# Attention's last product with one mask, gates in other tiles, pinned table loads and earlier kept weights in a two-layer hybrid kernel

## The chip, the cores and the metric

The kernel runs on one core of one Trainium2 chip. The metric is device time in microseconds (us) of the one launch. Engines are named as in the profile: PE (TensorE) does matrix products and transposes, PEld its weight loads, DVE is VectorE, ACT is ScalarE, POOL is GpSimd, SP is SyncE, which here does little but issue DMAs, in the order in which they stand in its program.

## The reference

One sequence of 512 tokens and width 1024 goes through two hybrid layers and one second block, all in float32. Cut to what matters here:

```python
def hybrid_layer(x, ...):
    h = rmsnorm(x, pre_mix_g)
    (dn_q, dn_k, dn_v, dn_z, dn_b, dn_a, sw_q, sw_k, sw_v,
     gate_a, gate_b) = jnp.split(h @ w_in, IN_OFFSETS, axis=-1)
    y_a = deltanet_branch(...) @ w_up_dn          # its output is gated by silu(z) as well
    y_b = swa_sink_branch(sw_q, sw_k, sw_v, positions, sw_sinks) @ w_up_sw
    mix = (sigmoid(gate_a) * y_a + sigmoid(gate_b) * y_b) @ w_o
    x = x + rmsnorm(mix, post_mix_g)
    h2 = rmsnorm(x, pre_mlp_g)
    ff = square(relu(h2 @ w_ff1)) @ w_ff2         # 4096 hidden
    return x + rmsnorm(ff, post_mlp_g)

# swa_sink_branch: 16 query heads, 2 key heads of 64, blocks of 128 tokens;
# every block sees itself and the block before it
off = qi - ki
in_band = (off >= 0) & (off < 128)
probs = p / (sum(p) + exp(sink - m))
o = einsum('bnhgqk,bnkhd->bnqhgd', probs, v_of_both_blocks)

# second block, state-space branch: tables of each group from parameters
dt = exp(log_dt); mag = exp(lam_re * dt); ang = lam_im * dt
bbar = coef(lam_re, lam_im, mag, ang) * (b_re, b_im)
```

The band has one property that the change uses: for a query row, the keys of the own block that are allowed (at or before it) and the keys of the block before that are allowed (after its place there) are complements. With the scores of both put in one 128-wide row, one probability matrix P holds both parts, and a mask says which part an entry belongs to.

## The kernel before

The token axis is the free axis of the products, and the 1024 channels lie as eight blocks of 128 partitions. Every float32 product is done as three matmuls on numbers split into a high and a low half (`mm3`; all matmuls are recorded at L78, transposes at L81). A weight block of 128x1024 is loaded by SP into a raw tile (`raw` has 2 buffers, `rawx` 1, `raws` its own), cast to its high half (`wh`, or `kw` where the block is kept for both halves of the tokens) by ACT at L241 or L221 (by POOL at L239), and the low half is a subtraction on DVE at L242 or L222.

A scheduler puts the instructions of each engine in an order, by costs that it estimates; an instruction passed to `tc.keep_in_program_order` keeps its place in the order in which the code is written. Each engine then works strictly in its order, and so does SP's queue of DMAs.

The stages of a layer that the change touches:

- Attention, L928 to L1025, a generator for each query block `b` and key head `kv`, run beside the projections. After the softmax (exponentials at L995, the scaling `sc` by `den` at L999), four heads at a time are transposed on PE and copied by ACT to `pc` (L1007). For b>0 POOL makes two masked copies of it, `pv` (L1010) for the values of the block before and `pc` in place (L1012) for the own values, and PE adds two products.
- Mix. For each of eight output blocks n, a load of the delta rule's output (`ogf`) and of its gate 0 (`gate`) from DRAM (`fetch`, L1315), their product on DVE (L1335), the split into `ah` (ACT L336, DVE L339); and the product of attention's output with `w_up_sw`, times gate 2 (L1340, `tb`). `ogf`, gate 0 and gate 2 take turns in one ring of three tiles ("fe"). Then follow the eight products that take all `ah`, with `w_up_dn`. Where a gate is not yet activated, ACT does it at L1321.
- Feed-forward. Its first product runs in two halves of 256 tokens; the residual and its norm are finished beside it (`xo` loads at L430, `xd_mid` stores at L401, `rt` on DVE and POOL at L432 and L433, `xsh`/`xsl` at L341/L342, squares summed in `sa` at L365/L370). The hidden blocks get relu and square on ACT (`ft` L1380, `fq` L1382) and a split (`hh` L336, `hl` L339). Beside it run `token_sums` (`tsa`, `tsb`) and `ssm_tables`, which loads the parameters of half of the second block's groups (`row` L1059, `dt` L1067, `lbr` and `lbi` L1072, `crow` L1105) and works out tables.
- Feed-forward's end. The last quarter of `w_ff2` is applied half by half: blocks 0 to 2 first by `halves3`, the other five by `dense_half`, each added to `acc` (L1490); the weights `kw` are kept for the second half.

Of the kernel before, what the change touches and what calls it, by code (L numbers as in the profile page):

```python
# [9 lines left out]
F32 = mybir.dt.float32  # L10
# [4 lines left out]
ALU = mybir.AluOpType  # L15
# [4 lines left out]
P = 128  # L20
# [3 lines left out]
KD = D // P  # L24
# [30 lines left out]
def body(  # L55
# [27 lines left out]
    T = Tensor()  # L83
# [16 lines left out]
    def rest(n):  # L100
        for _ in range(n):
            yield
# [119 lines left out]
            V.tensor_tensor(out=lo, in0=t, in1=f32(h), op=ALU.subtract)  # L222
            return h, lo

    def load_w(src, kn=KD, n=P, pool_h=False, keep=None):
        turn[0] += 1
        if turn[0] % 3 == 2 and turn[1] is not None and turn[0] > turn[2]:
            raw = turn[1].tile([P, kn, n], F32, tag="rawx", name="rawx", bufs=1)
        else:
            raw = wp.tile([P, kn, n], F32, tag="raw", name="raw", bufs=2)  # L230
        DMA.dma_start(out=raw, in_=src.rearrange("(k p) n -> p k n", p=P))
        h = lo = None
        if keep is not None:
            h, lo = keep(kn, n), keep(kn, n)
        if h is None:
            h = wp.tile([P, kn, n], F32R, tag="wh", name="wh", bufs=3)
            lo = wp.tile([P, kn, n], F32R, tag="wl", name="wl", bufs=3)
        if pool_h:
            G.tensor_scalar(out=h, in0=raw, scalar1=1.0, scalar2=0.0, op0=ALU.mult, op1=ALU.add)  # L239
        else:  # L240
            S.copy(out=h, in_=raw)  # L241
        V.tensor_tensor(out=lo, in0=raw, in1=f32(h), op=ALU.subtract)  # L242
        return h, lo

# [682 lines left out]
    def sw_item(l, b, kv, qk, vt, sw, kts, db):  # L927
# [70 lines left out]
        V.reciprocal(out=den, in_=den)  # L998
        V.tensor_tensor(out=sc, in0=sc, in1=den.unsqueeze(3).to_broadcast([P, 2, 4, P]), op=ALU.mult)  # L999
        yield from rest(PRB)  # L1000
        pcs = []
        for o in range(2):
            ps = ps_ax()
            for i in range(4):
                T.transpose(ps[:, i, :], sc[:, o, i, :], ident)
            pc, pv = sw.tile([P, 4, P], F32, tag="pc", name="pc", bufs=2), None
            S.copy(out=pc, in_=ps)  # L1007
            if b:
                pv = sw.tile([P, 4, P], F32, tag="pv", name="pv", bufs=2)
                G.affine_select(out=pv, in_=pc, pattern=[[0, 4], [-1, P]], base=0, channel_multiplier=1,  # L1010
                                compare_op=ALU.is_gt, fill=0.0)
            G.affine_select(out=pc, in_=pc, pattern=[[0, 4], [1, P]], base=0, channel_multiplier=-1,  # L1012
                            compare_op=ALU.is_ge, fill=0.0)
            pcs.append((pc, pv))
        yield from rest(PV)
        po = ps_ax()
        for o, (pc, pv) in enumerate(pcs):
            hs = slice(64 * o, 64 * o + 64)
            dst = po[hs].rearrange("p h t -> p (h t)")
            if b:  # L1020
                T.matmul(dst, lhsT=vt[:, b - 1, kv * 64:kv * 64 + 64], rhs=pv.rearrange("p h t -> p (h t)"), start=True, stop=False)
            T.matmul(dst, lhsT=vt[:, b, kv * 64:kv * 64 + 64], rhs=pc.rearrange("p h t -> p (h t)"), start=not b, stop=True)
        of = r2("sof")
        V.tensor_copy(out=of, in_=po)
        DMA.dma_start(out=db[:, 4 * kv:4 * kv + 4, b * P:(b + 1) * P], in_=of)  # L1025
# [20 lines left out]
    def ssm_tables(sp, hf):  # L1046
# [6 lines left out]

        prs = slice(NG * hf, NG * hf + NG)
        grs = slice(2 * NG * hf, 2 * NG * hf + 2 * NG)
        lam = {}
        for nm, src in (("lr", ssm_lam_re_2), ("li", ssm_lam_im_2)):
            row = sp.tile([NG, P], F32, tag="row", name="row")
            DMA.dma_start(out=row, in_=src[0, grs].rearrange("(i two) p -> i (two p)", two=2))  # L1059
            ps = ps_ax((P, NG))  # L1060
            T.transpose(ps, row, ident[:NG, :NG])
            lam[nm] = tl(nm)
            V.tensor_copy(out=lam[nm], in_=ps)
        lr, li = lam["lr"], lam["li"]
        dt = tl("dt")
        for half in range(2):
            DMA.dma_start(out=dt[64 * half:64 * half + 64, :],  # L1067
                          in_=ssm_log_dt_2[0, grs].rearrange("(i two) -> two i", two=2)[half].partition_broadcast(64))
        bre, bim = tl("lbr", (P, NG, 2, 16))[:, :, 0, :], tl("lbi", (P, NG, 2, 16))[:, :, 0, :]
        for dst, src in ((bre, ssm_b_re_2), (bim, ssm_b_im_2)):  # L1070
            for half in range(2):
                DMA.dma_start(out=dst[64 * half:64 * half + 64],  # L1072
                              in_=src[0, grs].rearrange("(i two) p c -> two p i c", two=2)[half])
        yield

# [26 lines left out]
        for src in (ssm_c_re_2, ssm_c_im_2):  # L1102
            crow = sp.tile([P, 2, 2, 64], F32, tag="crow", name="crow", bufs=2)
            for dup in range(2):
                DMA.dma_start(out=crow[:, :, dup, :], in_=src[0, grs].rearrange("(q g) c p -> (g c) q p", q=2))  # L1105
            crows.append(crow)
        s16 = (P, NG, 16)
        tC, tD = tl("tC", s16), tl("tD", s16)
# [83 lines left out]
    def layer(l, st, nxt):  # L1192
# [111 lines left out]
        with sbuf(f"mx{l}") as mp:  # L1304
            third(mp)
            def m2(name, dtype=F32R):
                t = mp.tile([P, 2, SEQ], dtype, tag="m2", name=name, bufs=NM2)
                return t[:, 0, :], t[:, 1, :]

            def keep(kn, n):  # L1310
                return mp.tile([P, kn, n], F32R, tag="m2", name="kw", bufs=NM2)

            def fetch(src, n, name):
                t = mp.tile([P, SEQ], F32, tag="fe", name=name, bufs=3)
                DMA.dma_start(out=t, in_=src[:, n, :])  # L1315
                return t

            def gate(i, n):
                t = fetch(dg[i], n, "gate")
                if (i, n) in plain:  # L1320
                    S.activation(out=t, in_=t, func=gate_fn[i])  # L1321
                return t

            bo, ao = [], []
            for n in range(KD):
                hl = m2("bh")
                split(*hl, fetch(db, n, "bf"), eng=G)
                bo.append(hl)
            tb = []
            for n in range(KD):  # L1330
                if n % 2 == 0:
                    pair = m2("tb", F32)
                w = load_w(w_up_sw[l][:, n * P:(n + 1) * P])
                t = fetch(og, n, "ogf")
                V.scalar_tensor_tensor(out=t, in0=t, scalar=pcol("dn_norm", l), in1=gate(0, n), op0=ALU.mult, op1=ALU.mult)  # L1335
                hl = m2("ah")
                split(*hl, t)
                ao.append(hl)
                ps = dense(w, bo)
                V.tensor_tensor(out=pair[n % 2], in0=ps, in1=gate(2, n), op=ALU.mult)  # L1340
                tb.append(pair[n % 2])
            mix = []
            for n in range(KD):
                ps = dense(load_w(w_up_dn[l][:, n * P:(n + 1) * P]), ao)
                ta_ = gate(1, n)
                V.tensor_tensor(out=ta_, in0=ps, in1=ta_, op=ALU.mult)
                V.tensor_tensor(out=ta_, in0=ta_, in1=tb[n], op=ALU.add)
                hl = m2("mh")
                split(*hl, ta_)
                mix.append(hl)  # L1350
            mo = [mt.tile([P, SEQ], F32, tag="mo", name="mo", bufs=KD) for _ in range(KD)]
            mid = Stream("pre_mlp", l * KD, f"xd_mid{l}", mt, False)
            wk, tick = {}, None
            for i in range(2):
                ms = Stats(mt)
                for n in range(KD):
                    if i == 0:
                        wk[n] = load_w(w_o[l][:, n * P:(n + 1) * P], keep=keep if n >= 3 else None)
                    ps = dense_half(wk[n], mix, i)
                    V.tensor_copy(out=mo[n][:, HALVES[i]], in_=ps)  # L1360
                    ms.add(mo[n][:, HALVES[i]])
                    if i:
                        tick()
                pending = residual(st, mo, ms.rstd, "post_mix", l * KD, mid, i)
                if i == 0:
                    before = pending
                    tick = ticks(before, AT_O)
            finish(before)

        with sbuf(f"ff{l}") as ff, ExitStack() as es2:  # L1370
# [109 lines left out]
            for i in range(2):  # L1480
                fs = Stats(tr)
                for n in range(KD):
                    if i == 0 and n == 0:
                        wk = {j: w.take() for j in range(3)}
                        head = halves3([wk[j] for j in range(3)], i)
                    elif i == 0 and n >= 3:
                        wk[n] = load_w(down(3, n)[0], keep=keep)
                    ps = head[n] if i == 0 and n < 3 else dense_half(wk[n], hid, i)
                    ac = acc[n][:, HALVES[i]]
                    V.tensor_tensor(out=ac, in0=ps, in1=ac, op=ALU.add)  # L1490
                    fs.add(ac)
                    if i:
                        tick()
# [275 lines left out]
```

## Time and profile before

| | us |
|---|---|
| median of 3 runs | 2309.17 (2308.73 to 2314.07) |
| the profiled execution | 2315.69 |
| its span, first to last instruction | 2313.9 |
| PE busy in it | 2243.0 (97%) |
| DVE busy | 1485.3 (64%) |
| ACT busy | 952.1 (41%) |
| POOL busy | 609.4 (26%) |
| DMA queue of SP (q1), share of 16 engines | 41.9% |

The profiled execution is 6.52 us longer than the median of the runs; 1.79 us of it lie outside the span. PE is the engine to look at: its weight loads overlap its matmuls, so its time is lost in two ways only, as idle time in front of an instruction that waits, and as stretches in which the granted clock is 0.5 of full speed (mean over the span 0.982).

### The profile page before, as it was taken

The numbers are of one execution on the slowest core, as the hardware profiler recorded it, in microseconds if no ns is written. First come the engines' busy times: TensorE is split into PE (matmuls) and PEld (weight loads), VectorE is DVE, ScalarE is ACT, GpSimd is POOL, SyncE is SP. The second block draws the span as 40 slices with busy tenths as digits, with TensorE's granted clock in tenths as the row PEclk, the third lists the DMA queues.
The fourth block names the chain that finished last, engine by engine and source line by source line (L and its number), as shares of the span: only waits on it lengthen the run. The fifth ranks groups of instructions, "written<-read, shape, count | busy, mean of one in ns | idle before, by whom it ended". The sixth has DMA issues, their size and how long they took to land. (4 is left out here: it accounts for less than half of the span.)

```text
span 2313.9 us, 37654 instructions
## 1 busy us (share of the span) xinstructions
PE 2243.0 (97%) x14460; PEld 1954.5 (84%) x14460; DVE 1485.3 (64%) x2958; ACT 952.1 (41%) x1726; POOL 609.4 (26%) x675
## 2 busy tenths in 40 slices
PE   8999999999999999999999999999999999899998
PEld 7867888887989899988678888889898898877788
DVE  5579793445576777665797934465777775435645
ACT  4554333333464354444533333334643444423333
POOL 1643420200336123246333202003351242200001
PEclk9999999999999999999999999999999999999999
DMA  5223424565453433342233345654434334563344
GB/s 177 62 72 87 101 83 128 172 200 160 121 157 92 128 107 98 116 125 58 77 87 88 92 127 182 201 164 126 136 101 118 114 97 123 169 165 117 108 131 146
DMA packets 466431, 284.33 MB, mean 123 GB/s; under 512 B 48502, under 2 KB 440012, under 8 KB 465740
## 3 DMA queue, kind: packets, MB, share of 16 engines
q1 hardware_dynamic: 462544, 280.69, 41.9%
q8 instruction: 114, 1.87, 0.3%
q10 hardware_dynamic: 3708, 1.24, 0.3%
q14 instruction: 65, 0.53, 0.1%
HBM read 235.76 MB, written 46.11 MB: 122 GB/s over the span
## 5 line engine op out<-in xcount | busy, mean ns | idle before, releaser
L78 PE MATMUL psm<-xsh,wh 128*128 128x512 f32 (+1 forms) x1136 | 445.6, 393 | 2.6 <-ACT wh L241 1.6
L78 PE MATMUL psm<-xsl,wh 128*128 128x512 f32 (+1 forms) x1136 | 432.6, 381 | 8.2 <-DVE xsl L342 4.2
L78 PE MATMUL psm<-xsh,wl 128*128 128x512 f32 (+1 forms) x1136 | 431.6, 380 | 0.0
L242 DVE TENSOR_TENSOR wl<-raw,wh 128x1024 fp32r<-128x1024 f32 (+2 forms) x179 | 213.3, 1192 | 89.9 <-ACT wh L241 63.6
L78 PEld LDWEIGHTS psm<-xsh,wh 128*128 128x128 f32 x1136 | 217.6, 192 | 48.4 <-issue 8.6
L78 PEld LDWEIGHTS psm<-xsl,wh 128*128 128x128 f32 x1136 | 218.1, 192 | 45.9 <-DVE xsl L342 5.5
L78 PEld LDWEIGHTS psm<-xsh,wl 128*128 128x128 f32 x1136 | 217.3, 191 | 40.9
L241 ACT CAST wh<-raw 128x1024 fp32r<-128x1024 f32 (+3 forms) x126 | 123.4, 980 | 253.6 <-PE psm L78 218.2
L370 POOL TENSOR_TENSOR sa<-sa,sq 128x256 f32<-128x256 f32 x54 | 51.5, 955 | 665.8 <-ACT sq L365 381.5
L78 PE MATMUL psm<-hh,wh 128*128 128x512 f32 (+1 forms) x480 | 177.1, 375 | 6.4 <-ACT hh L336 6.4
L78 PE MATMUL psm<-hl,wh 128*128 128x512 f32 (+1 forms) x480 | 177.7, 372 | 0.8 <-DVE hl L339 0.8
L78 PE MATMUL psm<-hh,wl 128*128 128x512 f32 (+1 forms) x480 | 176.7, 370 | 0.0
L221 ACT CAST wh<-raw 128x1024 fp32r<-128x1024 f32 x67 | 70.2, 1050 | 127.4 <-PE psm L78 76.2
L221 ACT CAST wh<-raws 128x1024 fp32r<-128x1024 f32 x63 | 66.0, 1047 | 127.9 <-PE psm L78 93.7
L222 DVE TENSOR_TENSOR wl<-raw,wh 128x1024 fp32r<-128x1024 f32 x67 | 97.4, 1454 | 26.0 <-ACT wh L221 23.5
L78 PEld LDWEIGHTS psm<-hh,wh 128*128 128x128 f32 x480 | 90.5, 191 | 22.8 <-ACT hh L336 7.0
L78 PEld LDWEIGHTS psm<-hl,wh 128*128 128x128 f32 x480 | 91.5, 191 | 16.4 <-DVE hl L339 1.3
L78 PEld LDWEIGHTS psm<-hh,wl 128*128 128x128 f32 x480 | 91.6, 191 | 15.1
L222 DVE TENSOR_TENSOR wl<-raws,wh 128x1024 fp32r<-128x1024 f32 x63 | 93.6, 1486 | 13.2 <-ACT wh L221 13.2
L239 POOL TENSOR_SCALAR wh<-raw 128x1024 fp32r<-128x1024 f32 (+1 forms) x53 | 62.9, 1186 | 121.0 <-PE psm L78 104.0
L78 PE MATMUL psm<-ah,wh 128*128 128x512 f32 x256 | 83.0, 405 | 5.2 <-ACT ah L336 5.0
L78 PE MATMUL psa<-xsh,wh 128*128 128x256 f32 x288 | 82.3, 286 | 0.0
(670 smaller groups left out, 5662.5 us busy)
## 6 DMA issues: line engine op xcount, KB each, us to landing
raw<-in_w_in_dram SPq DMA_DIRECT2D x130, 512.0 KB, 3.9
raw<-in_w_ff_dram SPq DMA_DIRECT2D x75, 512.0 KB, 4.1
raws<-in_w_ff_dram SPq DMA_DIRECT2D x51, 512.0 KB, 4.3
gate<-dg SPq DMA_DIRECT2D x48, 256.0 KB, 4.4
rawx<-in_w_in_dram SPq DMA_DIRECT2D x14, 512.0 KB, 4.1
raw<-in_w_up_sw_dram SPq DMA_DIRECT2D x12, 512.0 KB, 5.0
raw<-in_w_up_dn_dram SPq DMA_DIRECT2D x11, 512.0 KB, 4.5
raw<-in_w_o_dram SPq DMA_DIRECT2D x10, 512.0 KB, 4.7
```

The source lines that it names most:

```text
L78: return s.issue(nc.tensor.matmul(*a, **k))
L221: S.copy(out=h, in_=t)
L222: V.tensor_tensor(out=lo, in0=t, in1=f32(h), op=ALU.subtract)
L239: G.tensor_scalar(out=h, in0=raw, scalar1=1.0, scalar2=0.0, op0=ALU.mult, op1=ALU.add)
L241: S.copy(out=h, in_=raw)
L242: V.tensor_tensor(out=lo, in0=raw, in1=f32(h), op=ALU.subtract)
L370: (G if s.n in POOL_ACC else V).tensor_tensor(out=s.acc, in0=s.acc, in1=sq, op=ALU.add)
```

## The change

Four edits.

1. Attention, b>0: with P the unmasked probabilities, V_cur and V_prev the values of the own block and of the one before, and M(P) the part that belongs to the own block, the output is written as P V_prev + M(P) (V_cur - V_prev) in place of M'(P) V_prev + M(P) V_cur. The mask of `pc` in place goes (24 POOL instructions over the program; the 8 of b=0 stay), the 24 selects of `pv` carry the other mask, and 12 DVE subtractions `vd` of 128x64 are added. The number of matmuls is the same, and the product that takes the unmasked `pc` stands first.
2. Mix: gate 2 is loaded into tiles of another pool ("t2", 4 buffers) and no longer takes turns with `ogf` and gate 0.
3. `ssm_tables`: its loads keep the place on SP's queue that the code gives them.
4. Feed-forward's end: the kept weights of blocks 3 and 4 are loaded ahead of `halves3`, with the casts pinned in ACT's order, and each later one four blocks ahead.

```diff
-    def load_w(src, kn=KD, n=P, pool_h=False, keep=None):
+    def load_w(src, kn=KD, n=P, pool_h=False, keep=None, pin=False):
...
-            S.copy(out=h, in_=raw)
+            i = S.copy(out=h, in_=raw)
+            if pin:
+                tc.keep_in_program_order(i)
...
         yield from rest(PRB)
+        if b:
+            vd = sw.tile([P, 64], F32, tag="vd", name="vd", bufs=2)
+            V.tensor_tensor(out=vd, in0=vt[:, b, kv * 64:kv * 64 + 64], in1=vt[:, b - 1, kv * 64:kv * 64 + 64], op=ALU.subtract)
...
             S.copy(out=pc, in_=ps)
             if b:
                 pv = sw.tile([P, 4, P], F32, tag="pv", name="pv", bufs=2)
-                G.affine_select(out=pv, in_=pc, pattern=[[0, 4], [-1, P]], base=0, channel_multiplier=1,
-                                compare_op=ALU.is_gt, fill=0.0)
-            G.affine_select(out=pc, in_=pc, pattern=[[0, 4], [1, P]], base=0, channel_multiplier=-1,
-                            compare_op=ALU.is_ge, fill=0.0)
+                G.affine_select(out=pv, in_=pc, pattern=[[0, 4], [1, P]], base=0, channel_multiplier=-1,
+                                compare_op=ALU.is_ge, fill=0.0)
             pcs.append((pc, pv))
...
             if b:
-                T.matmul(dst, lhsT=vt[:, b - 1, kv * 64:kv * 64 + 64], rhs=pv.rearrange("p h t -> p (h t)"), start=True, stop=False)
-            T.matmul(dst, lhsT=vt[:, b, kv * 64:kv * 64 + 64], rhs=pc.rearrange("p h t -> p (h t)"), start=not b, stop=True)
+                T.matmul(dst, lhsT=vt[:, b - 1, vs], rhs=pr, start=True, stop=False)
+                T.matmul(dst, lhsT=vd, rhs=pv.rearrange("p h t -> p (h t)"), start=False, stop=True)
+            else:
+                T.matmul(dst, lhsT=vt[:, b, vs], rhs=pr, start=True, stop=True)
...
+        def queue(**k):
+            tc.keep_in_program_order(DMA.dma_start(**k))
+
...
-            DMA.dma_start(out=row, in_=src[0, grs].rearrange("(i two) p -> i (two p)", two=2))
+            queue(out=row, in_=src[0, grs].rearrange("(i two) p -> i (two p)", two=2))
...
             def gate(i, n):
-                t = fetch(dg[i], n, "gate")
+                if i == 2:
+                    t = t2("gate2")
+                    DMA.dma_start(out=t, in_=dg[i][:, n, :])
+                else:
+                    t = fetch(dg[i], n, "gate")
...
                         wk = {j: w.take() for j in range(3)}
+                        for j in (3, 4):
+                            wk[j] = load_w(down(3, j)[0], keep=keep, pin=True)
                         head = halves3([wk[j] for j in range(3)], i)
-                    elif i == 0 and n >= 3:
-                        wk[n] = load_w(down(3, n)[0], keep=keep)
+                    elif i == 0 and n + 4 < KD:
+                        wk[n + 4] = load_w(down(3, n + 4)[0], keep=keep)
```

The loads of `dt`, `lbr`, `lbi` and `crow` go through `queue` in the same way.

SP's queue in the mix of the first layer, before: `dg_201` is the DRAM tensor of gate 0, `dg_203` that of gate 2, `og_199` the delta rule's output, each load a block of 128x512.

```order
L1315 DMA gate<-dg_201 128x512
L1315 DMA gate<-dg_203 128x512
L1315 DMA ogf<-og_199 128x512
L231 DMA raw<-in_w_up_sw_dram 128x8x128
L1315 DMA gate<-dg_201 128x512
L1315 DMA gate<-dg_203 128x512
L1315 DMA ogf<-og_199 128x512
L231 DMA rawx<-in_w_up_dn_dram 128x8x128
```

And in the changed kernel, from the fifth load of gate 2 (`gate_5123`, the first that takes a tile used before) on:

```order
L1331 DMA gate_5123<-dg_203 128x512
L231 DMA raw<-in_w_up_sw_dram 128x8x128
L1325 DMA gate<-dg_201 128x512
L1325 DMA ogf<-og_199 128x512
L1331 DMA gate_5165<-dg_203 128x512
L1325 DMA gate<-dg_201 128x512
L231 DMA raw<-in_w_up_sw_dram 128x8x128
L1325 DMA ogf<-og_199 128x512
```

Gate 2 no longer stands between gate 0 and the next `ogf`; its loads are spread, and one of them stands in front of the load of a weight block.

SP's queue at the start of the first layer's feed-forward, before: the `raw` of the third row down to the `xd_mid` store are the stretch in question.

```order
L1067 DMA dt<-in_ssm_log_dt_dram 64x8x1 x2
L1072 DMA lbr<-in_ssm_b_re_dram 64x8x16
L231 DMA raw<-in_w_ff_dram 128x8x128
L1072 DMA lbr<-in_ssm_b_re_dram 64x8x16
L1072 DMA lbi<-in_ssm_b_im_dram 64x8x16
L189 DMA raw<-in_w_ff_dram 128x8x128
L1072 DMA lbi<-in_ssm_b_im_dram 64x8x16
L1105 DMA crow<-in_ssm_c_re_dram 128x2x64 x2
L1105 DMA crow<-in_ssm_c_im_dram 128x2x64 x2
L401 DMA xd_mid_5569<-rt 128x256
L430 DMA xo<-xd_in 128x256
L189 DMA raw<-in_w_ff_dram 128x8x128
```

In the changed kernel, the same place, and the place to which the loads of the tables went:

```order
L432 DMA xo<-xd_in 128x256
L231 DMA raw<-in_w_ff_dram 128x8x128
L189 DMA raw<-in_w_ff_dram 128x8x128 x2
L403 DMA xd_mid_5565<-rt 128x256
L432 DMA xo<-xd_in 128x256
```

```order
L321 DMA tsa<-xd_mid_5565 128x512
L321 DMA tsb<-xd_mid_5565 128x512
L1064 DMA row<-in_ssm_lam_im_dram 8x128
L1064 DMA dt<-in_ssm_log_dt_dram 64x8x1 x2
L1064 DMA lbr<-in_ssm_b_re_dram 64x8x16 x2
L1064 DMA lbi<-in_ssm_b_im_dram 64x8x16 x2
L189 DMA raws<-in_w_ff_dram 128x8x128 x2
```

The three `raw` and the residual's loads and stores now follow each other; `crow` comes once the residual is done, and `dt`, `lbr` and `lbi` stand between the second `row` and two loads of `raws`.

ACT at the end of the second layer's feed-forward, before: `kw` are the casts of kept weights, `ft`, `fq` and `hh` the last hidden blocks.

```order
L241 CAST kw<-raw 128x1024
L1380 ACTIVATE ft<-y_19689 128x512
L241 CAST kw<-raw 128x1024
L1382 ACTIVATE fq<-ft 128x512
L1380 ACTIVATE ft<-y_19688 128x512
L241 CAST kw<-raw 128x1024
L336 CAST hh<-fq 128x512
L1382 ACTIVATE fq<-ft 128x512
L336 CAST hh<-fq 128x512
L241 CAST kw<-raw 128x1024
L241 CAST kw<-rawx 128x1024
L365 ACTIVATE sa<-acc 128x256
```

The same place in the changed kernel:

```order
L1396 ACTIVATE fq<-ft 128x512
L1394 ACTIVATE ft<-y_19680 128x512
L338 CAST hh<-fq 128x512
L1396 ACTIVATE fq<-ft 128x512
L338 CAST hh<-fq 128x512
L241 CAST kw<-raw 128x1024 x2
L367 ACTIVATE sa<-acc 128x256
L367 ACTIVATE sq<-acc 128x256 x2
L241 CAST kw<-raw 128x1024
```

No cast of a kept weight stands between the steps of the last hidden blocks any more; in the first layer it is the same.

## Rows read from the trace of the kernel before

**Rows 1.** Waits of PE over the span: us in total, times, longest.

```profile
PE psm L78 <- ACT hh L336: 6.4, 2, 4.4
PE psa L78 <- POOL pv L1010: 6.3, 2, 3.2
PE psm L78 <- ACT ft L1380: 5.4, 2, 2.7
```

**Rows 2.** Windows: start:end, length, busy time of each engine, PE's clock, DMA, GB/s.

```profile
131.00:141.00 10.00, 6.72 (x30) 2.63 (x27) 5.04 (x8) 4.21 (x15) 4.47 (x5) 0.83 0.19 52
1110.00:1120.00 10.00, 6.86 (x26) 2.96 (x25) 4.94 (x8) 4.16 (x15) 4.47 (x5) 0.66 0.20 54
515.00:537.00 22.00, 18.58 (x67) 14.20 (x66) 13.22 (x17) 6.37 (x8) 0.00 (x0) 0.84 0.72 213
1504.00:1513.00 9.00, 6.56 (x21) 4.73 (x20) 6.24 (x8) 3.24 (x4) 0.00 (x0) 0.81 0.79 234
615.00:653.00 38.00, 31.98 (x233) 30.95 (x232) 22.26 (x42) 20.11 (x48) 14.10 (x18) 0.91 0.63 168
1597.00:1629.00 32.00, 27.13 (x184) 26.12 (x183) 18.30 (x34) 16.38 (x40) 12.33 (x14) 0.84 0.65 162
942.00:953.00 11.00, 8.04 (x41) 7.14 (x40) 5.77 (x9) 5.01 (x9) 0.73 (x1) 0.69 0.61 177
1918.00:1930.00 12.00, 7.00 (x39) 6.30 (x38) 6.42 (x8) 7.55 (x11) 0.34 (x1) 0.72 0.57 160
```

**Rows 3.** Timeline of attention in layer 0: start, duration, instruction [idle before <- releaser].

```profile
132.64 1.04 ACT L1007 COPY pc<-psa 128x512 f32<-128x512 f32 x2
133.20 1.22 DVE L999 TENSOR_TENSOR sc<-sc,den 128x1024 f32<-128x1024 f32 x1
133.27 2.24 POOL L1010 TENSOR_SCALAR_AFFINE_SELECT pv<-pc 128x512 f32<-128x512 f32 x2 [4.37 <-ACT pc L1007]
...
134.97 1.07 PE L78 MATMUL psa<-pv,vt__214 128*64 128x512 f32 x2 [3.18 <-POOL pv L1010]
...
135.46 1.22 POOL L1012 TENSOR_SCALAR_AFFINE_SELECT pc<-pc 128x512 f32<-128x512 f32 x2
```

**Rows 4.** Timeline of the mix in layer 0: ACT, DVE and PE.

```profile
501.20 1.05 ACT L241 CAST wh<-raw 128x1024 fp32r<-128x1024 f32 x1
...
522.03 0.75 DVE L1335 SCALAR_TENSOR_TENSOR ogf<-ogf,prm,gate 128x512 f32<-128x512 f32 x1 [3.28 <-DMA gate<-dg]
...
528.62 0.62 ACT L336 CAST ah<-ogf 128x512 fp32r<-128x512 f32 x1 [4.23 <-DVE ogf L1335]
...
529.29 0.80 PE L78 MATMUL psm<-ah,wh 128*128 128x512 f32 x1 [2.78 <-ACT ah L336]
```

**Rows 5.** Timeline of the feed-forward in layer 0: SP's queue, ACT and DVE.

```profile
621.31 0.41 SPq L231 DMA_DIRECT2D raw<-in_w_ff_dram  x1
621.76 5.75 SPq L1072 DMA_DIRECT2D lbr<-in_ssm_b_re_dram  x1
...
633.02 1.04 ACT L241 CAST kw<-raw 128x1024 fp32r<-128x1024 f32 x1 [10.42 <-DMA raw<-in_w_ff_dram]
...
673.12 6.21 SPq L189 DMA_DIRECT2D raws<-in_w_ff_dram  x2
...
684.50 0.28 DVE L1030 TENSOR_TENSOR A<-cor,lbr 128x128 f32<-128x128 f32 x1
...
692.07 1.05 ACT L221 CAST wh<-raws 128x1024 fp32r<-128x1024 f32 x1 [4.38 <-PE psm L78]
```

**Rows 6.** DMA issues of the page: KB each, median us from issue to landing.

```profile
raw<-in_w_ff_dram SPq DMA_DIRECT2D x75, 512.0 KB, 4.1
```

**Rows 7.** Timeline of ACT at the end of both layers' feed-forward.

```profile
943.95 1.04 ACT L241 CAST kw<-raw 128x1024 fp32r<-128x1024 f32 x1 [1.26 <-DMA raw<-in_w_ff_dram]
...
1919.52 1.04 ACT L241 CAST kw<-raw 128x1024 fp32r<-128x1024 f32 x1 [1.64 <-DMA raw<-in_w_ff_dram]
```

More of the change, by code (lines that the diff above doesn't have):

```diff
@@ L1019, in sw_item @@
             dst = po[hs].rearrange("p h t -> p (h t)")
+            pr = pc.rearrange("p h t -> p (h t)")
+            vs = slice(kv * 64, kv * 64 + 64)
             if b:
-                T.matmul(dst, lhsT=vt[:, b - 1, kv * 64:kv * 64 + 64], rhs=pv.rearrange("p h t -> p (h t)"), start=True, stop=False)
-            T.matmul(dst, lhsT=vt[:, b, kv * 64:kv * 64 + 64], rhs=pc.rearrange("p h t -> p (h t)"), start=not b, stop=True)
+                T.matmul(dst, lhsT=vt[:, b - 1, vs], rhs=pr, start=True, stop=False)
+                T.matmul(dst, lhsT=vd, rhs=pv.rearrange("p h t -> p (h t)"), start=False, stop=True)
+            else:
+                T.matmul(dst, lhsT=vt[:, b, vs], rhs=pr, start=True, stop=True)
         of = r2("sof")
@@ L1066, in ssm_tables @@
         for half in range(2):
-            DMA.dma_start(out=dt[64 * half:64 * half + 64, :],
+            queue(out=dt[64 * half:64 * half + 64, :],
                           in_=ssm_log_dt_2[0, grs].rearrange("(i two) -> two i", two=2)[half].partition_broadcast(64))
@@ L1071, in ssm_tables @@
             for half in range(2):
-                DMA.dma_start(out=dst[64 * half:64 * half + 64],
+                queue(out=dst[64 * half:64 * half + 64],
                               in_=src[0, grs].rearrange("(i two) p c -> two p i c", two=2)[half])
@@ L1104, in ssm_tables @@
             for dup in range(2):
-                DMA.dma_start(out=crow[:, :, dup, :], in_=src[0, grs].rearrange("(q g) c p -> (g c) q p", q=2))
+                queue(out=crow[:, :, dup, :], in_=src[0, grs].rearrange("(q g) c p -> (g c) q p", q=2))
             crows.append(crow)
```

## The prediction

> **What bounds the kernel now.** The page's busy times come first: PE is busy for 97% of the span, so what can be had is PE's idle time and the time that it loses at half clock. The view of PE's waits is next. Among its longest are attention's masked copy `pv`, 6.3 us in all, the hidden block `ft`, 5.4, and `hh`, 6.4, each twice, once in each layer [rows 1]; the split block `ah` in the mix is a fourth, 2.78 in layer 0 [rows 4]. Then the windows around these eight stalls: length less PE's busy time is idle time, and what PE's clock lacks of 1.00, times the length, is what the clock took [rows 2]. The clock is at one of two levels, 2.4 or 1.2 GHz, and these windows show that each stall has a stretch at 1.2 GHz with it. Idle plus clock, layer 0 and layer 1:
>
> - attention: 3.28 + 1.70 and 3.14 + 3.40, together 11.5 us
> - mix: 3.42 + 3.52 and 2.44 + 1.71, together 11.1 us
> - start of the feed-forward: 6.02 + 3.42 and 4.87 + 5.12, together 19.4 us
> - end of the feed-forward: 2.96 + 3.41 and 5.00 + 3.36, together 14.7 us
>
> That is 56.8 us, 2.5% of the time. It is an upper bound, since idle time at half clock is counted twice. Each of the four edits stands at one of these places. The last view is the timeline of each, to see what the wait hangs on.
>
> **Attention.** Two `pc` copies of ACT end at 133.68, and the four selects of POOL behind them stand one after another: `pv` twice in 2.24, `pc` twice in 1.22, ending at 136.68. PE idles for 3.18 until 134.97 [rows 3], that is from 131.79. With the change the first `pc` copy stands ahead of the exponentials in ACT's order, so the first half of the heads has both its inputs before 131.79 and PE can use that time. The second half waits for its copy, at about 133.7 as now since ACT does the same work, and for one select instead of two. A select takes 0.61 in the pair of L1012; in the pair of L1010, whose first one alone fits before DVE's L999 (133.20 to 134.42), the two took 2.24, so one of them took about 1.6.
> The Trainium skill has a rule for this, in "SBUF — State Buffer", section "🔬 SBUF: two separate sides": a DVE instruction with two SBUF inputs and a GpSimd instruction that reads SBUF exclude each other for their whole length. The trace agrees (L999 reads two tiles in SBUF, and a select beside it lost about 1.0 us). The rule speaks against the gain, since the second select still falls into L999, and ends at about 135.0 rather than 134.3; by it the two layers give 6 us, without it 7.2.
> In rows alone: the second half's last input comes at 135.0 in place of 136.68, and the first half no longer shares the wait, so PE gets through this place 2 to 3 us earlier per layer, and the stretch at half clock may go as well. The 12 subtractions `vd` are not in the trace; the nearest row, a DVE instruction of 128x128 from two tiles, takes 0.28 [rows 5], so at most 12 x 0.28 = 3.4 us of DVE, and nothing at the least, where DVE has room. Bounds of the part: -3.4 to +11.5. I take 6, near the row of the selects.
>
> **Mix.** The last multiplication but one of `ogf` with its gate starts at 522.03, after 3.28 us in which DVE waits for the load of the gate; the last `ah` cast is at 528.62, and PE waits 2.78 for it [rows 4]. The chain is a ring: gate 0 takes the tile that gate 2 left, gate 2 is free only when PE's product has been multiplied, so the loads for a block start only as PE ends an earlier one. With gate 2 elsewhere `ogf` and gate 0 have three tiles for themselves and run a block or more ahead: a block of PE is 24 matmuls, at 18.58 us for 67 [rows 2] some 6.7 us, against the 2.78 that is missing. What is late next is the weights: the cast at 501.20 is for the block that PE starts at 529.29, 28 us ahead, so they are not. Bounds 0 and 11.1; I take 8.5, which leaves a short wait and one half-clock stretch of those two.
>
> **Start of the feed-forward.** `raw` is issued at 621.31, and the loads of `lbr`, `lbi` and `crow` go beside it and behind it on SP; one `lbr` holds the queue for 5.75. ACT sits idle for 10.42 until `raw` has landed, and casts it at 633.02 [rows 5], 11.7 us after its issue; the median of this load is 4.1 [rows 6]. All behind this cast on ACT (`ft`, on which PE waits 2.7, `xsh`) and behind those loads on SP (the residual's `xo` and `xd_mid`) is late by up to 11.7 - 4.1 = 7.6 us. With the loads moved, the cast comes at about 625.4, 7.6 us earlier, more than each wait of PE there. What is late next is the residual's own chain, with its loads in front of or between the weight loads. At most 19.4 can go; I take 14, for some of the short waits (`xsl`, `sa`) and one half-clock stretch may stay.
> The cost of the move: the same loads now stand in front of `raws`, issued so far at 673.12 and cast at 692.07, which is 14.8 us more than the 4.1 that it needs. The four of `lbr` and `lbi` at 5.75 each would be 23.0, 8.2 over that slack; at the 11.7 by which they held up `raw` they fit. So the cost is 0 to 8.2 us per layer, and I take 0. The cover besides is DVE, which needs `lbr` at 684.50 [rows 5], 11 us after the place where the loads now go. Bounds of the part: -16.4 to +19.4.
>
> **End of the feed-forward.** The cast of a kept weight at 943.95 waits 1.26 for its load, that at 1919.52 waits 1.64, and both stand ahead of `fq` and `hh` of the last hidden blocks on ACT [rows 7]; PE's two waits on `hh` are 4.4 and, from the total of 6.4, 2.0 [rows 1]. In the changed order no cast stands between them, so a late load holds nothing that PE needs first. The load of a kept weight is issued earlier too, and blocks 3 and 4 are wanted only once `halves3` has run. Next late is the sum into `acc` and the fourth block's low half on DVE, about 0.5 us per layer. Bounds 0 and 14.7; I take 10.5, since half of the clock's 6.8 counts idle time again.
>
> **The sum.** 6 + 8.5 + 14 + 10.5 = 39 us. The profiled execution would go from 2315.69 (span 2313.9) to 2276.7 (2274.9). It stood 6.5 us above the median of the runs; what that is the trace of one execution can't tell, so I take the same 39 off the median, from 2309.17 to 2270.
>
> **Rivals.**
>
> - *Next-late waits take half.* Every stall is one of a chain, and with DVE and POOL at work beside it another operand is late: the second `pc` and its select, the residual's `xsl`, the sums of `acc`. For it: short waits stand behind the long ones in the same windows, as 2.96 us of idle time [rows 2] against 2.0 on `hh` [rows 1]. Against it: the moved casts and loads come 7 us and more early where PE lacks under 4.5. Half of 39 is 19.5, time 2290.
> - *The idle time goes, the half clock stays.* For it: in layer 1 attention lost 3.40 to the clock and in layer 0 1.70 after the same idle time [rows 2], so the length of a wait alone doesn't set it. Then only idle time counts: of the windows' 31.1 some 23, time 2286. Against it: every one of these stretches has a stall in its window.
> - *Slower: gate 2's loads hold the weights.* In the changed queue each of the last four gate-2 loads of a layer waits until the product four blocks earlier has been multiplied, and a weight block stands behind it. Were this wait the last, each of the 8 would cost PE a landing, a cast and a subtraction, at least 4.1 [rows 6] + 1.05 [rows 4] + about 1.2, so 6.4 us, 51 us in all; less the other three parts (30.5) the time would be 2330. It decides from the point at which PE's lead over its weights falls under 6.4 us; the row of 501.20 shows 28. The same holds for the tables, at up to 8.2 us per layer.
> - *The change does not do what it says*: the scheduler is free in all but the pinned places, and waits move elsewhere for no gain. 2309.
>
> **How the numbers follow.** Forecast 0.62, its own range 2260 to 2281 (28 to 49 us saved). Half 0.18, idle time alone 0.12, no change 0.04, slower 0.04. The range that should hold the time 8 times in 10 runs from 2257, where nearly all that the windows show is saved and the rest untouched, to 2294, which takes in both partial cases. Faster by over 0.3%, which is 6.9 us and about what a measurement of this kernel can tell from no change: 0.92. Within it 0.04, slower 0.04.
>
> **What would show it.** Attention: POOL's L1010 pair down to one select per half, PE's wait on `pv` under 1.5 us per layer. Mix: no wait on `ah` and the last `ah` cast some us ahead of PE. Start of the feed-forward: `raw` landing within 5 us of its issue, ACT's idle 10.42 gone, PE's waits on `ft` gone, and no wait on `raws` at 690 to 700. End: no wait on `hh` over 1 us. In the windows of the same stages PE's clock is 1.00. I am wrong if PE's waits fall and the mean clock doesn't rise, if new waits of over 2 us stand behind the old ones, or if SP's queue shows a weight load late behind `gate` or `lbi`.

## The result and the profile after

The changed kernel takes 2272.51 us (median of 4 runs, 2269.41 to 2275.94) against 2309.62 in the same comparison: a ratio of 0.9836, interval 0.9817 to 0.9855, so 37.1 us less. The forecast was 2270, 39 less.

The profiled execution took 2269.41 with a span of 2267.7, the lowest of the four, while that of before, 2315.69, lay above all runs of its kernel; so the two traces differ by 46.2 us of span, 9 more than the medians. The first part of the page splits that in two; its columns are busy time, share of the span and count.

```profile
span 2267.7 us, 37630 instructions
PE 2219.0 (98%) x14460; PEld 1937.1 (85%) x14460; DVE 1486.3 (66%) x2970; ACT 945.1 (42%) x1722; POOL 585.9 (26%) x643
```

The same 14460 matmuls took 24.0 us less of PE's time, and PE's idle time fell from 70.9 to 48.7, by 22.2. Less busy time for the same work is the clock: its mean went from 0.982 to 0.993. So between these two executions about half of the difference is clock. For the medians the share is smaller: the profiled execution of before has the lowest mean clock on record of that kernel (37 others lie between 0.983 and 0.990, their mean is 0.987), and the four of the changed kernel have 0.991 to 0.993. By these means the clock gives back about 0.6% of the time, an estimate of 13 us, a third of the 37.

POOL has 643 instructions where it had 675. All 32 selects of `pc` went, the 8 of b=0 too, which the list of the edits counts as staying: the new code has no mask there.

The waits of PE in the changed kernel, in us in total, times and longest, against [rows 1]:

```profile
PE psm L78 <- DVE xsl L341: 7.2, 6, 2.0
...
PE psa L78 <- DVE y L312: 3.3, 2, 1.6
PE psm L78 <- DVE wl L244: 3.1, 6, 1.1
...
PE psa L81 <- DVE na L691: 2.1, 2, 1.1
...
PE psm L78 <- DVE acc L1506: 1.6, 2, 0.8
PE psa L78 <- POOL pv L1015: 1.3, 2, 0.7
```

No wait on `hh`, `ft` or `ah` is left, and that on `pv` went from 6.3 to 1.3. Two are new: on `y` (not there before), 1.6 in each layer, and on `na`, 1.1 in each. The one on `wl` grew from 1.2 to 3.1. The 7.2 on `xsl` were there before, at places that no edit touches.

The windows of the same stages in the changed kernel, to be laid beside [rows 2] in the same order (attention, mix, start of the feed-forward and its end, each twice):

```profile
127.00:134.50 7.50, 6.85 (x37) 4.07 (x36) 3.54 (x6) 7.02 (x23) 3.58 (x4) 1.00 0.27 72
1083.00:1093.00 10.00, 9.35 (x46) 5.51 (x45) 6.04 (x10) 6.99 (x23) 4.37 (x4) 1.00 0.20 55
511.00:527.00 16.00, 15.87 (x71) 12.82 (x70) 10.92 (x15) 4.30 (x5) 0.00 (x0) 1.00 0.68 208
1475.00:1481.00 6.00, 6.00 (x28) 4.95 (x28) 4.28 (x6) 1.68 (x2) 0.00 (x0) 1.00 0.87 258
605.00:635.00 30.00, 29.15 (x240) 28.54 (x239) 22.00 (x44) 21.16 (x50) 14.46 (x18) 1.00 0.70 206
1564.00:1589.00 25.00, 23.29 (x189) 22.50 (x188) 18.05 (x34) 16.85 (x42) 12.51 (x15) 1.00 0.63 182
921.00:931.00 10.00, 9.20 (x78) 9.03 (x77) 7.19 (x13) 7.22 (x12) 1.38 (x1) 1.00 0.32 93
1874.00:1884.00 10.00, 9.22 (x77) 9.04 (x76) 7.19 (x15) 6.71 (x12) 0.00 (x0) 1.00 0.27 79
```

PE's clock (the column behind POOL's) is 1.00 in all of them, where it was 0.66 to 0.91: with each stall its stretch at 1.2 GHz went too, also where a wait of 0.6 to 1.0 us stayed. Around the new waits on `wl`, `y` and `na` the clock is 1.00 as well.

### The profile page after: what moved, and what is told of

It reads as the page before. It is cut to its first block, busy times and chain, and to the rows that moved or that the text cites. A ratio compares the mean times of both kernels' runs of the same rounds, so it can differ in the third digit from the quotient of the medians.

```text
span 2267.7 us, 37630 instructions
## 1 busy us (share of the span) xinstructions
PE 2219.0 (98%) x14460; PEld 1937.1 (85%) x14460; DVE 1486.3 (66%) x2970; ACT 945.1 (42%) x1722; POOL 585.9 (26%) x643
## 5 line engine op out<-in xcount | busy, mean ns | idle before, releaser
L78 PE MATMUL psa<-xsl,wh 128*128 128x256 f32 x288 | 81.4, 283 | 0.0
```

Source lines behind the costliest of these rows:

```text
L78: return s.issue(nc.tensor.matmul(*a, **k))
```

## The experiments

Each kernel was timed beside the kernel before, whose median was 2308.7 to 2309.1 in these comparisons.

| kernel | median us | ratio to before, interval |
|---|---|---|
| edit 1 alone (attention) | 2301.36 | 0.9970 (0.9961 to 0.9980) |
| edit 2 alone (gates) | 2303.00 | 0.9974 (0.9962 to 0.9985) |
| edit 3 alone (tables) | 2297.53 | 0.9952 (0.9933 to 0.9971) |
| edit 4 alone (kept weights) | 2294.97 | 0.9941 (0.9921 to 0.9960) |
| before, `dt` in larger pieces | 2291.77 | 0.9932 (0.9914 to 0.9950) |
| before, gate 0 out of the ring | 2298.86 | 0.9958 (0.9946 to 0.9970) |
| change, casts not pinned | 2282.45 | 0.9883 (0.9865 to 0.9902) |
| change, `dt` in larger pieces | 2265.89 | 0.9815 (0.9801 to 0.9830) |
| the same, gate 0 out, not gate 2 | 2263.26 | 0.9803 (0.9789 to 0.9816) |
| the same, tables not pinned | 2262.25 | 0.9796 (0.9783 to 0.9810) |
| change, `dt`, both gates out | 2262.96 | 0.9801 (0.9788 to 0.9814) |

**Each edit alone.** Each kernel is the kernel before with the lines of the diff that belong to one edit.

> Edit 1 alone on the kernel before. Theory (each edit acts at its own place and the gains add): PE's waits on pv fall from 6.3 us to about 1.3 and the wait on pc goes, the half-clock stretches of attention go, and nothing changes elsewhere: about 8 us less, 2301. Rival (the gain is a by-product of the scheduler's other order and shows only with all four edits): within 3 us of before, or a gain of over 4 us outside attention.

> Edit 2 alone on the kernel before. Theory (own place, gains add): no wait on ah at the end of the mix, both half-clock stretches there gone, some 2 us of new waits on wl in the first layer as in the changed kernel: 9 us less, 2300. Rival (gains need the other edits): within 3 us of before.

> Edit 3 alone on the kernel before. Theory (own place, gains add): the weight load at the start of the feed-forward lands within 5 us of its issue, waits on ft and xsl there go, 8 us less per layer; 1.6 us per layer given back some 100 us later at y, where the tables' work on POOL is late: 13 us less in all, 2297. Rival (gains need the other edits, or the late tables cost the same in whatever kernel is slower): under 6 us less, 2303 or more.

> Edit 4 alone on the kernel before. Theory (own place, gains add): PE's waits on hh, 6.4 us, go, 0.8 us per layer on acc stays, both half-clock stretches gone: 11 us less, 2298. Rival (the other order that the scheduler gives to the rest moves other waits): less than half of it, 2304 or more.

By the medians they save 7.3, 5.7, 11.2 and 13.7 us, together 37.9, where the change saves 37.1: as far as such medians can tell the gains add, and none is a by-product of the others. The waits that go are those that were named: in the run of edit 4 alone no wait on `hh` stands in PE's list, in that of edit 3 alone the `y` of 3.2 is there already, and in that of edit 1 alone the `na` of 2.1. The gates gave less than the 9 expected, the kept weights more than the 11; with intervals of some 4 to 9 us across, only that each gains is certain from the times. Edit 1 takes away a mask and also puts the product of the unmasked `pc` first; what each of the two is worth was not tried.

**Casts not pinned.** The changed kernel with

```diff
-                            wk[j] = load_w(down(3, j)[0], keep=keep, pin=True)
+                            wk[j] = load_w(down(3, j)[0], keep=keep)
```

> The changed kernel without the pin on the casts of kept weights 3 and 4; they are still loaded ahead of halves3. The scheduler then puts the casts ahead of the last hidden blocks on ACT again. Theory A (the order of the casts is what counts): waits on hh come back, with half-clock stretches, 5 to 11 us more than the changed kernel, 2278 to 2284. Theory B (the earlier loads count, so that no cast waits for its load): waits on hh under 1 us, within 3 us of the changed kernel.

It took 2282.45, 10 more than the change, and PE's wait on `hh` is back at nearly its old size:

```profile
PE psm L78 <- ACT hh L338: 5.8, 2, 4.1
```

ACT in that kernel shows why, with the casts of kept weights and the last two `hh` (start, duration, instruction):

```profile
925.04 0.62 ACT L338 CAST hh<-fq 128x512 fp32r<-128x512 f32 x1
...
927.31 1.05 ACT L241 CAST kw<-raw 128x1024 fp32r<-128x1024 f32 x1 [1.12 <-DMA raw<-in_w_ff_dram]
...
928.92 0.62 ACT L338 CAST hh<-fq 128x512 fp32r<-128x512 f32 x1
...
930.04 1.05 ACT L241 CAST kw<-raw 128x1024 fp32r<-128x1024 f32 x1 [0.50 <-DMA raw<-in_w_ff_dram]
```

The cast at 927.31 still waits for its load, and `hh` stands behind it. So it is the pin, that is the place of the casts on ACT, that removed this stall; theory A holds. The earlier loads were not put to the test, because none is earlier. Counted from the same `ft` on ACT (930.99 before, 914.61 without the pin, 914.13 in the changed kernel, all in the first layer), SP issues three of the five loads at the same places in all three kernels, to 0.3 us. The other two it issues 8.8 and 10.3 us after that `ft` before, 8.8 and 10.5 without the pin, and only from 13.7 on in the changed kernel. The stall went although these loads came later.

**What held up `raw`.** The prediction laid the late landing of `raw` to the loads of `lbr`, `lbi` and `crow`. The window view of the kernel before says otherwise; columns as above, the last two are the DMA engines' share and GB/s.

```profile
617.80:627.60 9.80, 9.17 (x78) 8.97 (x77) 5.08 (x9) 4.24 (x8) 3.83 (x5) 1.00 0.04 1
627.60:633.00 5.40, 4.10 (x35) 3.89 (x33) 0.00 (x0) 0.00 (x0) 0.00 (x0) 1.00 0.86 165
```

For 9.8 us the DMA engines moved 1 GB/s, and for the last 6.3 of them `raw` was already issued (621.31). Ahead of `raw` in the queue stood one `lbr` and `dt`: 1024 values of 4 bytes, each to a place of its own. Its row in the kernel before, KB and us to landing:

```profile
dt<-in_ssm_log_dt_dram SPq DMA_DIRECT2D x2, 2.0 KB, 7.7
```

So `dt` alone was changed: 16 neighbouring values to every partition, in pieces of 64 bytes, of which ACT's exponential takes every other one. The code moves no load; the scheduler now puts both `lbr` and one `lbi` ahead of `raw`, where it was one `lbr`.

```diff
-        for half in range(2):
-            DMA.dma_start(out=dt[64 * half:64 * half + 64, :],
-                          in_=ssm_log_dt_2[0, grs].rearrange("(i two) -> two i", two=2)[half].partition_broadcast(64))
...
+        DMA.dma_start(out=dt16.rearrange("p i two -> p (i two)"), in_=ssm_log_dt_2[0, grs].partition_broadcast(P))
...
-        tc.keep_in_program_order(S.activation(out=dt, in_=dt, func=AF.Exp))
...
+            tc.keep_in_program_order(S.activation(out=dt[hs], in_=dt16[hs, :, half], func=AF.Exp))
```

> The kernel before, its loads where they were, with one thing changed: dt is loaded as 128 pieces of 64 B (16 neighbouring values to every partition) and picked apart by ACT's exponential, in place of 1024 pieces of 4 B. Theory A (the 4-byte pieces ahead of raw in the queue hold it up; DMA moves only some 10 GB/s in the 10 us after them): raw lands within 6 us of its issue, the waits on ft go and most of edit 3's gain comes without moving anything, 9 to 13 us less, 2297 to 2300. Theory B (lbr, lbi and crow behind and beside raw hold it up): raw still lands 10 us or more after its issue and the time is within 4 us of before.

It took 2291.77, 17 us less than the kernel before: more than theory A expected, and by the medians more than moving the loads gave (11.2), though the two intervals overlap. PE's waits on `ft` are 2.8 in four, the longest 0.9, where they were 5.4 in two. The landing of `dt`, and then SP's queue and ACT in that kernel (start, duration, instruction):

```profile
dt<-in_ssm_log_dt_dram SPq DMA_DIRECT2D x1, 8.0 KB, 2.5
```

```profile
613.62 0.35 SPq L1066 DMA_DIRECT2D dt<-in_ssm_log_dt_dram  x1
614.02 1.38 SPq L1070 DMA_DIRECT2D lbr<-in_ssm_b_re_dram  x2
615.44 0.63 SPq L1070 DMA_DIRECT2D lbi<-in_ssm_b_im_dram  x1
617.16 0.38 SPq L231 DMA_DIRECT2D raw<-in_w_ff_dram  x1
...
621.26 1.05 ACT L241 CAST kw<-raw 128x1024 fp32r<-128x1024 f32 x1 [2.83 <-DMA raw<-in_w_ff_dram]
```

Twice the bytes of the two loads together land in a third of the time; `lbr` holds the queue for 1.38 for both of its halves, where one took 5.75 [rows 5]; and `raw`, still behind `dt`, both `lbr` and an `lbi`, is cast 4.1 us after its issue, where it was 11.7. Theory B is out: `lbr` and `lbi` were victims like `raw`. The pieces became both larger and fewer; which of the two did it was not tried.

In the changed kernel the same pieces sit where the loads were moved to.

> The changed kernel with dt loaded as 128 pieces of 64 B as above. Theory A: ACT's wait of 2.6 us for dt goes, the tables start about 3 us earlier on DVE and POOL, and PE's wait on y (1.63 us in each layer) goes: 2 to 4 us less than the changed kernel, about 2269.5. Theory B (the tables are late for other reasons): wait on y stays over 1 us, time within 1 us of the changed kernel.

ACT in the changed kernel, at the exponential of `dt`:

```profile
663.72 1.28 ACT L1086 ACT_TABLE_LOAD   x1 [2.62 <-DMA dt<-in_ssm_log_dt_dram]
```

and with the larger pieces, with no wait:

```profile
660.74 1.28 ACT L1086 ACT_TABLE_LOAD   x1
```

The wait on `y` is gone from PE's list there, as theory A said. The median is 2265.89, 6.6 under the change, with no run of the one among those of the other; the spans of the two profiled executions differ by only 2.4 (2265.3 against 2267.7), so how much of the 6.6 is the run-to-run spread stays open.

**Which tile leaves the ring.** The kernel before with gate 0 in the other tiles in place of gate 2:

```diff
-                if i == 2:
-                    t = t2("gate2")
+                if i == 0:
+                    t = t2("gate0")
```

(the difference to edit 2).

> The kernel before with gate 0 in the other tiles in place of gate 2; ogf and gate 2 share the ring of three. Theory (what matters is that gate 2 is tied to PE's product of its block and that ogf takes its place): the wait on ah stays, 1 to 3 us per layer, gain under 4 us. Rival (the ring is only too small, whichever tile leaves it): the wait on ah goes as with gate 2, 7 to 9 us less, about 2301.

2298.86, and no wait of PE on `ah` or on anything else from 480 to 530; so the theory that gate 2's tie to PE's product is the point falls, and the rival, a ring too small for three, holds. In that stretch edit 2 alone has one wait, 1.5 on `wl`, and the change has these two, in us in total, times and longest:

```profile
PE psm L78 <- DVE wl L244: 2.0, 2, 1.1
```

DVE's order in the changed kernel shows where it is from:

```profile
504.94 0.75 DVE L1349 SCALAR_TENSOR_TENSOR ogf<-ogf,prm,gate 128x512 f32<-128x512 f32 x1 [4.18 <-DMA gate<-dg]
505.61 1.22 DVE L244 TENSOR_TENSOR wl<-raw,wh 128x1024 fp32r<-128x1024 f32 x1
```

The low half of a weight block stands behind a multiplication that waits 4.18 for gate 0, and PE, which waits for that low half at 506.02, stands 0.87. With gate 2 out, gate 0 is still loaded into the ring and its wait still stops the weights, as it did once before the change, for 0.64. Whether gate 0 is the better one to move, the times alone don't settle: the intervals of the two kernels overlap.

**Together.** Three versions, all with `dt` in 64-byte pieces and edits 1 and 4.

> The changed kernel with dt in 64-byte pieces and with gate 0 rather than gate 2 in the other tiles. Theory (gains are of separate places and add; ogf with gate 2 in the ring leaves no wait on wl): 4.6 us, by which gate 0 alone beat gate 2 alone, less than 2265.9, so 2261; no wait on ah, wl in the mix. Rival (what gate 0 gained alone is lost where PE is earlier): 2265 or more.

> As all_gate0, but the tables' loads are not pinned (edit 3 undone; dt in 64-byte pieces). Theory (with dt mended the place of these loads costs nothing and their move gains nothing): within 3 us of all_gate0, about 2260 by the gains measured alone (7.3 + 10.3 + 17.4 + 13.7 off 2308.9). Rival (the other loads, some 4000 pieces of 64 B and 128 KB of crow, still hold up raw or the residual): 4 us or more slower than all_gate0, waits on ft or xsl at the start of the feed-forward.

> As all_gate0, but gate 0 and gate 2 both in the four other tiles, ogf alone in the ring. Theory (ring too small for three, any relief does): within 3 us of all_gate0. Rival (gate 0 and gate 2 now take turns with each other in four tiles, and tie gate 0 to PE's product again): waits on ah or wl in the mix, 3 to 9 us slower.

They took 2263.26, 2262.25 and 2262.96, within 1 us of each other, and each is faster than the kernel before and than the change; the lowest is 0.9796 of before (0.9783 to 0.9810). For all_gate0 the step of 2.6 from 2265.89 lies within the spread, so neither its theory nor its rival is shown by the time; the wait on `wl` is 0.3 in its list in place of 2.9. The second says most: with `dt` mended the tables' loads can stand where the scheduler puts them, so the gain of edit 3 is gone, within what these runs can tell. Some of what its rival named is back: two waits on `ft`, 1.8 in all, the longest 1.1. The third is as its theory said.

## Why the prediction was right, point by point

The four places were the right ones, and each part of the sum lies within the interval that its own edit measured. That the total came within 3 us of the measured time is luck beside that: by the medians the runs gave 1.3 us more, 2.8 less, 2.8 less and 3.2 more than the parts, which cancel, and the clock's share was read off the execution with the lowest clock on record. In the mix and at the start of the feed-forward steps of the working failed.

- **Attention**, 6 forecast. Edit 1 alone gave 7.3 (4.6 to 9.0 by its interval). The second select still falls into DVE's multiplication, as forecast. By the rule of the Trainium skill that the prediction names ("SBUF — State Buffer", section "🔬 SBUF: two separate sides") the two instructions exclude each other; the trace agrees:

```profile
132.52 1.22 DVE L1001 TENSOR_TENSOR sc<-sc,den 128x1024 f32<-128x1024 f32 x1
...
132.59 1.65 POOL L1015 TENSOR_SCALAR_AFFINE_SELECT pv<-pc 128x512 f32<-128x512 f32 x1 [3.40 <-ACT pc L1012]
...
134.29 1.07 PE L78 MATMUL psa<-pv,vd 128*64 128x512 f32 x2 [0.65 <-POOL pv L1015]
```

  1.65 against 0.64 for the first one, which stands alone at 127.52. In the kernel before it was the first select of the pair that stood beside L999 (133.27 against 133.20 in [rows 3]), not the second, as the prediction reads it; the 1.6 are the same. PE waits 0.65 for it per layer, under the 1.5 that was set as the mark. Not foreseen: PE arrives earlier at the next stage and waits 1.1 there for DVE's `na`. A `vd` took at most 0.22, under the bound of 0.28, except for one of the twelve, which took 0.60.
- **Mix**, 8.5 forecast, 5.7 alone (3.5 to 8.8). The wait on `ah` and both half-clock stretches went, as forecast. Three things were wrong. The first is "28 us ahead, so they are not" of the weights. The cast at 501.20 belongs to an earlier block: PE stands at 529.29 inside its first product with `ah`, which begins at 521.59 and takes the weights that ACT casts at 515.84. The low half on DVE comes later still, and for the block before PE already had to wait for one:

```profile
515.84 1.04 ACT L241 CAST wh<-rawx 128x1024 fp32r<-128x1024 f32 x1
...
516.47 0.50 PE L78 MATMUL psm<-bh,wl 128*128 128x512 f32 x1 [0.64 <-DVE wl L242]
...
517.53 1.22 DVE L242 TENSOR_TENSOR wl<-rawx,wh 128x1024 fp32r<-128x1024 f32 x1
...
521.59 0.62 PE L78 MATMUL psm<-ah,wh 128*128 128x512 f32 x2
```

  So the lead was 5.8 us at the start of the cast and 4.1 at that of the low half, and in the changed kernel the low half stood behind the wait for gate 0, and PE with it for 2.0 us in the first layer. The second is that `ogf` and gate 0 "run a block or more ahead": DVE still waits 4.18 for gate 0 at 504.94. The third is the mechanism, that gate 2 is the one tile that must leave; it fell with the run of gate 0.
- **Start of the feed-forward**, 14 forecast, 11.2 alone (6.7 to 15.5). `raw` is cast 4.0 us after its issue, PE's wait on `ft` is gone, `xsl` there is down to 1.0. The step that failed is the naming of the cause, `lbr`, `lbi` and `crow`, and with it the cost of the move, taken as 0 because they were priced at 11.7 us of queue against 14.8 of slack. `dt` was not priced at all; moved along, it landed late for ACT by 2.62, the tables on DVE and POOL followed, and some 60 us later PE waited 1.63 per layer on `y`. That lies inside the stated bound of 0 to 8.2 per layer.
- **End of the feed-forward**, 10.5 forecast, 13.7 alone (9.2 to 18.2). The step held, casts behind `hh`, and PE waits 0.8 per layer on `acc` against the 0.5 forecast. "The load of a kept weight is issued earlier too" did not come about: no load is earlier, in the first layer two are later, and the stall went all the same.
- **The clock.** Of the rivals "the idle time goes, the half clock stays" was the one to fear, at 2286. Every stretch at one of the eight places went with its stall. But a stall does not always bring the same stretch. PE's first wait on `pv` is 3.15 to 3.18 us in the six traces that have it; the clock took 1.7 us around it in five and 3.4 in that of edit 2 alone. Of the 38 stalls of 1.4 to 4.3 us that stayed at these places in the traces of the other kernels, three have no stretch at 1.2 GHz within the 9 us behind them, such as the 2.13 on `ah` in layer 1 with edit 3 alone. So the 25.6 us that the windows lost to the clock are the figure of one execution, and what decides over it stays open.
- **Slower, by gate 2's loads in front of weights.** Those loads did not hold a weight load long enough for PE to stand; what stood was DVE, behind gate 0. The rival was nearer than the prediction has it, since it decides under a lead of 6.4 us and the lead was 5.8, not 28.

## What to carry to other kernels

When a large load lands late, look at how much the DMA engines moved meanwhile: here a nearly idle stretch led to the small pieces ahead of it in the queue. Reshaping those few bytes did at least as well as moving them, since the load that was moved as it was made ACT wait at its new place. On an engine that works in the order of its program, a wait is one of all that stands behind it. So for a stall the cheap cures here were the place of the late instruction in the order (the pin was worth 10 us) and one tile fewer in a ring that was too small for three; a larger ring was not tried. When a gain is put down to an earlier load, look whether the load is earlier: here it was not. A stall of 2 to 4 us at these places mostly cost 1.7 or 3.4 us in clock besides, and sometimes nothing, so such waits are worth hunting in a kernel whose PE is busy for 97%, but one execution does not tell the clock's part of the gain.

## What was not expected of the hardware

Two loads of 2 KB in 4-byte pieces, 1024 in all, took 7.7 us to land. Meanwhile the DMA engines moved 1 GB/s for 9.8 us, with a load of 512 KB waiting behind them for the last 6.3; in the 5.4 us after that they moved 165 GB/s. The same values in 128 pieces of 64 bytes, 8 KB with every value written twice, landed in 2.5 us.
